# Recurrence of a linear-attention layer: squares of x in mid-chunk, roots by four, w_o loaded in part during the gate stage, seven PSUM banks for v and gate, the inverses' operand stored in their own order

## The chip, the cores and the metric

One core of one Trainium2 chip runs the whole program. The metric is device time in microseconds (us) of one execution.

## What is computed

A decoder trunk of two layers on x of 1024 tokens by 1024 channels, all in float32. The change lies in the first layer's time mixing, which works on the normalised input h with 16 heads of 64:

```python
x_r, x_w, x_k, x_v, x_a, x_g = h[None] + (x_prev - h)[None] * mu          # six mixes
r, k, v = x_r @ W_r, x_k @ W_k, x_v @ W_v
g = sigmoid(x_g @ g1) @ g2
def step(S, inp):                                 # for each token and head
    sa = einsum('bhvk,bhk->bhv', S, -kk_t)
    S = S * w_t + sa * b_t + v_t * k_t
    return S, einsum('bhvk,bhk->bhv', S, r_t)
...
y = groupnorm(y) * lnx_w + lnx_b
x = x + ((y + bonus) * g) @ w_o                   # residual
# next: h = rmsnorm(x), the first layer's MLP, ...
```

## The kernel before

The recurrence over 1024 tokens is done as 16 chunks of 64 tokens. Within a chunk the delta rule becomes a triangular system, whose 32x32 diagonal blocks are inverted beforehand. The order of the work is written out for most of the recurrence (`keep_in_program_order` pins an instruction to its engine's program order); in the projections a scheduler that simulates a timeline orders what is not pinned.

Up to about 230 us, the k projection (L824 products) runs beside *units* of preparation. Eight pairs of units, `prep_pair`, each make two 128x8x64 blocks of the matrix N (A_ab) from products of KK and BK, and SP stores each whole to the DRAM tensor `d_N` (L270, 256 KB, runs of 2 KB). `d_E`, `d_KR` and `d_BK` hold other prepared operands, of which `prep_receptance` loads `Er` and `kr` (L278, L281) again in the r projection (230 to 318 us, also L824).

`prep_inverse(b)`, b = 0 and 1, inverts half of the diagonal blocks each on DVE: 31 steps of two operations (L314, L316) on tiles `Nb`, `Tb`, `Tm`. Its operand `Nb` is gathered from `d_N` by 32 loads of 32 KB with runs of 128 bytes (L306), on the ACT queue for b = 0 and on SP for b = 1. The inverses stand beside the r projection (b = 0) and the v projection (L844, 318 to 417 us, b = 1). `mix(j)` makes the two halves (hi on ACT L730, lo on DVE L733) of a mixed input for each projection. The v projection's and the gate's products go to four PSUM banks (tile `mm`, pool `ps`); `psA`, three banks, is used by the units.

After the gate's first products (422 to 446 us) the recurrence runs. Chunk c solves (`pp`, copied by ACT to `Ps` L475, then `sa`, then `Z` on DVE L487), updates the state (`u`), makes its output `yp`, normalises and gates it, while blocks of the next chunk are prepared between. From chunk 3 on 24 products of w_o are filled into each chunk; they add a row block of 128 tokens (`xt`, L605) every second chunk. ACT then squares the row (L612, sum into `ssx`) and `rsqrt_small` makes the row's root (five DVE operations, L85 to L91, two ACT ones); both are issued after the second product of the next row, which places them ahead of `Ps` in chunks 5, 7, 9, 11, 13, 15 and once at the end.

A counter, `hook`, is called about seven times a chunk (hooks 0 to 6 before chunk 0, 7 to 13 in chunk 0, and so on) and lets other work in: steps of the gate's second product (table `GS`; tiles `gp`, copied by ACT L1124, stored to `d_g` by SP L1126), and the eight 128x1024 pieces of w_o. Piece i is loaded at hook 5 + 2i, and three hooks later ACT casts it (`woh`, L581) and POOL takes the difference (`wol`, L582). All eight thus fall in chunks 0 to 2.

Of the kernel before, what the change touches and what calls it, by code (L numbers as in the profile page):

```python
# [562 lines left out]
def stage_recurrence(k, a, tile_of, gates):  # L563
    nc, tc = k.nc, k.tc
    with ExitStack() as ctx:
        rec_pools(k, ctx, a)
# [8 lines left out]
        def load_wo(i):  # L575
            raw = k.rzz.tile([P, D], F32, tag="woraw", name="woraw", bufs=3)
            for q, hs in enumerate(HALF):
                tc.keep_in_program_order(nc.sync.dma_start(raw[hs], wv[i // 2, i % 2, q]))
# [4 lines left out]
            wo.append((hi, lo))
        xt, zs = [], []

        def w_out():

            done = None
            for tt in range(NK):
                zh, zl = zs[tt]  # L590
                for e in range(2):
# [14 lines left out]
                    if e == 1 and tt < NK - 1:  # L606
# [3 lines left out]
                        def done(tt=tt, zl=zl):  # L610
                            ss = k.rw.tile([P, 1], F32, tag="ssx", name="ssx")
                            nc.scalar.activation(zl.rearrange("p a b -> p (a b)"), xt[tt], AF.Square, accum_out=ss)  # L612
                            rsqrt_small(k, k.rw, k.rstd[tt], ss, 1.0 / D, 1e-6, tag="x")
# [14 lines left out]
        hooks, loads = 0, []  # L628
# [1463 lines left out]
```

## Time and profile before

| | us |
|---|---|
| three runs: lowest, median, highest | 2640.52, 2641.9, 2645.92 |
| the profiled execution: its time / its span | 2639.1 / 2637.4 |
| busy in the span: PE, DVE, ACT, POOL | 2537.5, 1852.2, 1237.6, 507.5 |
| recurrence, first to last chunk's products (462.13 to 757.89) | 295.76 |

The mean granted clock of TensorE is 0.983. PE is busy for 96% of the span, so time can only come from its gaps and from stretches at a lower clock. Lines of the first view below are stretches; a row of a timeline gives the start, the duration and, in brackets, for how long the engine was idle and what ended it.

### The profile page before, as it was taken

How to read it: one execution, taken by the hardware profiler on the slowest of the kernel's cores; microseconds unless marked ns; L12 is line 12 of the kernel's file. 1: busy time of each engine (PE TensorE's matmuls, PEld its weight loads, DVE VectorE, ACT ScalarE, POOL GpSimd, SP SyncE). 2: the span in 40 equal slices, each digit the busy share in tenths (PEclk: the TensorE clock that was granted, in tenths of full speed). 3: DMA queues.
4: the chain of work that ended last, by engine and by line, in shares of the span. 5: the costliest groups of instructions: out<-in, count | busy, mean ns of one | idle time of the engine just before them, and what ended most of it. 6: DMA issues, size and time to landing. Idle time of an engine off the chain costs nothing.

```text
span 2637.4 us, 44718 instructions
## 1 busy us (share of the span) xinstructions
PE 2537.5 (96%) x17601; PEld 2141.5 (81%) x17601; DVE 1852.2 (70%) x2982; ACT 1237.6 (47%) x2136; POOL 507.5 (19%) x395
## 2 busy tenths in 40 slices
PE   7999998799999999999999899999999999999999
PEld 4887897677778888888888899887887888878887
DVE  6665965788868777566778768587736877746675
ACT  4763324422355555443455424588715555543332
POOL 2011222866620000000301122344300000000020
PEclk9999999899999999999999999999999999999999
DMA  4468654966425544666641321755341644376664
GB/s 129 126 168 189 169 131 145 231 162 164 114 66 164 169 139 160 250 227 240 229 147 65 118 76 64 209 137 148 87 152 48 208 163 144 131 264 220 224 212 141
DMA packets 413510, 417.51 MB, mean 158 GB/s; under 512 B 189482, under 2 KB 297218, under 8 KB 413300
## 3 DMA queue, kind: packets, MB, share of 16 engines
q1 hardware_dynamic: 394068, 392.50, 49.0%
q0 software_dynamic: 4128, 12.66, 1.3%
q10 hardware_dynamic: 15104, 9.51, 1.2%
q8 instruction: 138, 2.26, 0.4%
q14 instruction: 72, 0.59, 0.1%
HBM read 292.76 MB, written 121.82 MB: 157 GB/s over the span
## 4 chain that ended last, share of the span: by engine, by line
PE 69%; DVE 15%; DMA 6%; issue 4%; ACT 3%; POOL 2%; SPq 1%; POOLq 0%; DVEq 0%; ACTq 0%
PE mm L365 34%; PE mm L768 7%; PE mm L766 7%; PE mm L767 7%; PE mm L824 4%; PE tp L368 2%; PE wo L365 1%; DVE Tb L316 1%; DMA b<-d_c 1%; PE s L365 1%; DVE Tm L314 1%; PE z1p L1001 1%; DVE AE L427 1%; PE o L365 1%; DMA R<-d_sm 1%
## 5 line engine op out<-in xcount | busy, mean ns | idle before, releaser
L365 PE MATMUL mm<-ol,oh 128*128 128x512 f32 x896 | 349.9, 391 | 1.3 <-DVE ol L733 1.3
L365 PE MATMUL mm<-oh 128*128 128x512 f32 x896 | 349.7, 390 | 1.3 <-ACT oh L730 1.3
L365 PE MATMUL mm<-oh,ol 128*128 128x512 f32 x896 | 349.9, 390 | 0.5 <-DVE ol L733 0.3
L730 ACT CAST oh<-ra 128x1024 fp32r<-128x1024 f32 x108 | 113.8, 1054 | 335.8 <-PE mm L365 237.5
L733 DVE TENSOR_TENSOR ol<-ra,oh 128x1024 fp32r<-128x1024 f32 x108 | 137.8, 1276 | 123.6 <-ACT oh L730 123.4
L365 PEld LDWEIGHTS mm<-ol,oh 128*128 128x128 f32 x896 | 168.9, 188 | 36.9 <-DVE ol L733 1.7
L365 PEld LDWEIGHTS mm<-oh,ol 128*128 128x128 f32 x896 | 168.9, 188 | 36.5 <-DVE ol L733 1.4
L365 PEld LDWEIGHTS mm<-oh 128*128 128x128 f32 x896 | 168.8, 188 | 36.5 <-ACT oh L730 1.7
L766 PE MATMUL mm<-xhT,ah 128*128 128x512 f32 x448 | 174.3, 389 | 0.0
L767 PE MATMUL mm<-xlT,ah 128*128 128x512 f32 x448 | 174.3, 389 | 0.0
L768 PE MATMUL mm<-xhT,al 128*128 128x512 f32 x448 | 174.3, 389 | 0.0
L1495 POOL DMA_DIRECT2D xt<-d_xh x8 | 4.4, 552 | 755.1 <-DMA rb<-in_mlp_w_out_dram 421.4
L730 ACT CAST ah<-w 128x512 fp32r<-128x512 f32 x128 | 79.3, 621 | 113.5 <-PE mm L767 102.1
L766 PE MATMUL mm<-xhB,ah 128*128 128x512 f32 x336 | 130.7, 389 | 0.0
L767 PE MATMUL mm<-xlB,ah 128*128 128x512 f32 x336 | 130.7, 389 | 0.0
L768 PE MATMUL mm<-xhB,al 128*128 128x512 f32 x336 | 130.7, 389 | 0.0
L733 DVE TENSOR_TENSOR ol<-rb,oh 128x1024 fp32r<-128x1024 f32 x92 | 120.8, 1313 | 2.1 <-ACT oh L730 1.8
L1811 ACT ACTIVATE l<-l,mx 128x512 f32<-128x512 f32 (+7 forms) x128 | 99.2, 776 | 34.3 <-DVE mx L1808 34.1
L1268 ACT ACTIVATE z<-z 128x512 f32<-128x512 f32 x112 | 70.8, 633 | 68.9 <-DVE z L1265 67.3
L767 PEld LDWEIGHTS mm<-xlT,ah 128*128 128x128 f32 x448 | 84.1, 188 | 17.6
L730 ACT CAST oh<-rb 128x1024 fp32r<-128x1024 f32 x92 | 96.4, 1048 | 4.0 <-DMA rb<-in_mlp_w_out_dram 4.0
L768 PEld LDWEIGHTS mm<-xhT,al 128*128 128x128 f32 x448 | 84.1, 188 | 17.4
(487 smaller groups left out, 6952.6 us busy)
## 6 DMA issues: line engine op xcount, KB each, us to landing
rb<-in_mlp_w_out_dram SPq DMA_DIRECT2D x124, 512.0 KB
ra<-d_H SPq DMA_DIRECT2D x108, 512.0 KB
w<-in_mlp_w_in_dram SPq DMA_DIRECT2D x64, 512.0 KB
d_H<-z SPq DMA_DIRECT2D x56, 512.0 KB
d_H<-sums SPq DMA_DIRECT2D x32, 768.0 KB
raw<-in_rwkv_w_rkv_dram SPq DMA_DIRECT2D x24, 512.0 KB
KRz<-d_KR SPq DMA_DIRECT2D x16, 512.0 KB
KRz<-d_BK SPq DMA_DIRECT2D x16, 512.0 KB
```

The costliest lines, as they stand in the source:

```text
L314: nc.vector.tensor_tensor(Tm[:, :, 0:n, 0:m], Nb[:, :, j, j + 1:32].unsqueeze(3).broadcast_to(S), Tb[:, :, j:j + 1, 0:m].broadcast_to(S), ...
L316: nc.vector.tensor_tensor(Tb[:, :, j + 1:32, 0:m], Tb[:, :, j + 1:32, 0:m], Tm[:, :, 0:n, 0:m], op=ALU.add)
L365: return self.tc.keep_in_program_order(self.tc.nc.tensor.matmul(*args, **kw))
L368: return self.tc.keep_in_program_order(self.tc.nc.tensor.transpose(*args))
L730: nc.scalar.copy(hi, src)
L733: lo_eng.tensor_tensor(lo, src, hi.bitcast(F32), op=ALU.subtract)
L766: te.matmul(out, ah, bh, start=i == 0, stop=False)
L767: te.matmul(out, ah, bl, start=False, stop=False)
L768: te.matmul(out, al, bh, start=False, stop=i == n - 1)
L824: nc.tensor.matmul(o[e][half], wt[:, i % 4, es], xs[i][part][:, 512 * half:512 * half + 512], start=i == 0 and wt is hi and part == 0, sto ...
L1268: nc.scalar.activation(x, x if o is None else o, AF.Relu)
L1811: nc.scalar.activation(l, l, AF.Exp, bias=m, scale=-1.0, accum_out=SM[:, j, qb:qb + 1])
```

## The change

- `d_N` becomes two tensors in the order in which `Nb` lies. `prep_pair` stores only the diagonal blocks, by eight stores of 32x8x32 (runs of 128 bytes) instead of two; `Nb` is one load on SP.
- The v products and the gate's first products rotate over seven banks (three of `psA`, four of `ps`).
- w_o's pieces follow a table `WO` of hooks. Pieces 1, 2, 3 have a pool of their own, the raw data of two of them is loaded in the gate stage, and they are converted at hooks 1, 3 and 5, ahead of chunk 0. Pieces 0, 5, 6 have their difference on POOL (hooks 10, 17, 24), 4 and 7 on DVE (hooks 21, 28).
- ACT loads its table at hook 9 instead of ahead of the `gp` copies, and stores `d_g` on its own queue.
- The squares of a row are issued once a chunk, between the state update and `rec_out`; roots are taken for rows 0 to 3 at once and for 4 to 6 at once.

```diff
-W0, WS, WL = 5, 2, 3
+WO = {1: (0, 1), 2: (0, 3), 3: (3, 5), 0: (5, 10), 4: (9, 16, 21), 7: (12, 23, 28), 5: (14, 17), 6: (18, 24)}
+EARLY = [1, 2, 3]
...
-    k.d_N = [dr.tile([P, HC, C], F32, name=f"d_N{i}") for i in range(2 * NK)]
+    k.d_N = [dr.tile([2, P, 32, 32], F32, name=f"d_N{i}") for i in range(2)]
...
-        nc.sync.dma_start(k.d_N[2 * p + h], N_)
+        u = 2 * (p % 4) + h
+        for c in range(2):
+            for d in range(2):
+                s0 = u % 4 * 32 + (c * 2 + d) * HC
+                q = 64 * c + 32 * d
+                nc.sync.dma_start(k.d_N[p // 4][u // 4, s0:s0 + HC].rearrange("c i t -> i c t"),
+                                  N_[q:q + 32, :, 32 * d:32 * d + 32])
...
-                (nc.sync if b else nc.scalar).dma_start(Nb[s0:s0 + HC, u // 4],
-                                  k.d_N[8 * b + u][q:q + 32, :, 32 * d:32 * d + 32].rearrange("i c t -> c i t"))
+    nc.sync.dma_start(Nb, k.d_N[b].rearrange("g s i t -> s g i t"))
...
-                            if done and (i, q) == (1, 2):
-                                done()
...
+        def squares():
+            while late:
+                tt, zl = late.pop(0)
+                tc.keep_in_program_order(nc.scalar.activation(zl..., xt[tt], AF.Square, accum_out=ss[:, tt:tt + 1]))
+                if tt in (3, 6):
+                    n = tt % 4 + 1
+                    rsqrt_small(k, k.rw1, k.rstd4[tt // 4][:, 0:n], ss[:, tt + 1 - n:tt + 1], 1.0 / D, 1e-6, tag=f"x{tt}")
...
+            if hooks == 9:
+                tc.keep_in_program_order(nc.scalar.preload_act_table_set("natural_log_exp_and_others"))
...
                     St = rec_state(k, cur, Z, Zn, St)
+            squares()
             rec_out(k, cur, Z)
...
-        fill(48)
+        fill(6)
+        squares()
+        fill(42)
+        k.wo_early.close()
...
+        def bank():
+            pool, tag = (k.psA, "psA") if next(turn) % 7 < 3 else (ps, "mm")
+            return pool.tile([P, 512], F32, tag=tag, name="mm")
...
+    k.woraw = [wo_raw(k, a, k.woe, i, 2, tc.keep_in_program_order) for i in EARLY[:2]]
...
-    pin(nc.scalar.preload_act_table_set("natural_log_exp_and_others"))
...
-                    nc.sync.dma_start(k.d_g[...], t)
+                    nc.scalar.dma_start(k.d_g[...], t)
```

ACT in a chunk in which a row of x is complete, before (`TT`: copies for the solve; `zl<-xt` the square; `rs_t`, `rstd` the root; `BKt`: copies for the state update; `ysq`: the squares of the normalisation):
```order
L464 COPY TT_4250<-op_6234 32x4x32 x4
L612 ACTIVATE zl,ssx<-xt_5230 128x1024
L475 COPY Ps<-pp 128x512
L86 ACTIVATE rs_t<-rs_v 128x1
L87 ACTIVATE rstd_72<-rs_t 128x1
L435 COPY BKt<-tp 128x512 x2
L533 ACTIVATE ysq<-Y 128x512
```
and in the same chunk of the change:
```order
L466 COPY TT_4230<-op_6200 32x4x32 x4
L477 COPY Ps<-pp 128x512
L437 COPY BKt<-tp 128x512 x2
L598 ACTIVATE zl,ssx<-xt_5205 128x1024
L535 ACTIVATE ysq<-Y 128x512
```
The square moved from ahead of `Ps` to behind both `BKt` copies, and the two root operations are gone from this chunk.

ACT from the gate's first half to chunk 0's `Ps`, before (`gp` is the product of the gate's second half):
```order
L1109 ACT_TABLE_LOAD
L1124 COPY xt_4302<-gp 128x512 x2
L435 COPY BKt<-tp 128x512
L1124 COPY xt_4322<-gp 128x512 x2
L1124 COPY gs<-gp 128x512
L435 COPY BKt<-tp 128x512
L1124 COPY gs<-gp 128x512 x4
L447 COPY O_4394<-op 128x128
L1124 COPY gs<-gp 128x512
L464 COPY TT_4247<-op_4420 32x4x32 x4
L475 COPY Ps<-pp 128x512
```
and the same place in the change:
```order
L1156 COPY xt_4283<-gp 128x512 x2
L437 COPY BKt<-tp 128x512
L1158 DMA d_g<-xt_4283 128x2x512
L1156 COPY xt_4307<-gp 128x512 x2
L1158 DMA d_g<-xt_4307 128x2x512
L584 CAST woh_4297<-woraw 128x1024
L1156 COPY gs<-gp 128x512
L437 COPY BKt<-tp 128x512
L1156 COPY gs<-gp 128x512
L1158 DMA d_g<-gs 128x2x512
L584 CAST woh_4299<-woraw 128x1024
```
The table load is gone from here, and three stores of `d_g` and the first two casts of w_o pieces stand among the `gp` copies.

DVE at the first inverse, before (`Er`, `kr`: the r projection's results; `KK<-np`: the last pair's N):
```order
L269 TENSOR_TENSOR KK<-np__2120,nt 128x512
L269 TENSOR_TENSOR KK<-np__2121,nt 128x512
L291 TENSOR_TENSOR Er<-mm,Er 128x8x64
L292 SCALAR_TENSOR_TENSOR kr<-Er,cols_443,kr 128x512
L291 TENSOR_TENSOR Er<-mm,Er 128x8x64
L292 SCALAR_TENSOR_TENSOR kr<-Er,cols_443,kr 128x512 x3
L291 TENSOR_TENSOR Er<-mm,Er 128x8x64 x2
L314 TENSOR_TENSOR Tm<-Nb,Tb 128x2x31
L316 TENSOR_TENSOR Tb<-Tb,Tm 128x2x31
L314 TENSOR_TENSOR Tm<-Nb,Tb 128x2x30x2
```
and in the change:
```order
L299 TENSOR_TENSOR Er<-mm,Er 128x8x64
L246 TENSOR_TENSOR Em<-kt,Em 128x512
L248 TENSOR_TENSOR BK<-Em,BK 128x8x64
L250 TENSOR_TENSOR BK<-Em,a 128x8x64
L316 TENSOR_TENSOR Tm<-Nb,Tb 128x2x31
L243 SCALAR_TENSOR_TENSOR KK<-kt,cols_429,E_593 128x512
L318 TENSOR_TENSOR Tb<-Tb,Tm 128x2x31
L316 TENSOR_TENSOR Tm<-Nb,Tb 128x2x30x2
L318 TENSOR_TENSOR Tb<-Tb,Tm 128x2x30x2
```
The first step on `Nb` came forward from behind the r projection's `Er` results to the middle of the last pair's units, ahead of its N.

## Rows read from the trace of the kernel before

**Rows 1.** Stretches of the recurrence, one from each chunk's first state product `pp` to the next chunk's: chunks 0 to 5, 7, 9, 11, 13 and the last. Columns: stretch, its length, then busy us and instructions of PE, PE's weight loads, DVE, ACT and POOL, the granted clock, the DMA share and GB/s.
```profile
462.13:477.07 14.94, 12.76 (x249) 10.29 (x240) 10.31 (x14) 6.15 (x13) 8.66 (x7) 0.90 0.97 243
477.07:497.82 20.75, 14.80 (x276) 12.24 (x277) 16.01 (x23) 8.94 (x19) 19.43 (x14) 0.91 1.03 240
497.82:520.90 23.08, 17.78 (x286) 15.20 (x277) 17.72 (x25) 7.75 (x18) 20.08 (x16) 0.73 1.00 222
520.90:537.86 16.96, 16.61 (x299) 13.69 (x293) 14.50 (x24) 5.10 (x14) 11.71 (x10) 0.97 0.75 219
537.86:553.76 15.90, 15.90 (x293) 13.11 (x293) 14.04 (x25) 4.70 (x14) 10.27 (x9) 1.00 0.54 132
553.76:573.75 19.99, 16.68 (x294) 13.49 (x293) 17.45 (x30) 5.87 (x18) 13.41 (x12) 1.00 0.66 188
...
589.65:608.83 19.18, 16.52 (x294) 13.42 (x293) 16.69 (x28) 5.64 (x16) 12.92 (x13) 1.00 0.68 194
...
624.73:643.81 19.08, 16.57 (x294) 13.48 (x293) 16.61 (x28) 5.46 (x16) 13.51 (x13) 1.00 0.61 167
...
659.71:679.58 19.87, 17.66 (x293) 14.61 (x293) 16.61 (x30) 6.60 (x20) 13.24 (x13) 0.91 0.51 136
...
696.38:714.68 18.30, 16.52 (x293) 13.42 (x293) 15.76 (x30) 6.56 (x20) 11.40 (x11) 1.00 0.39 89
...
730.58:757.89 27.31, 23.13 (x209) 18.77 (x208) 14.89 (x32) 7.61 (x18) 9.04 (x7) 0.88 0.07 16
```

**Rows 2.** Waits of PE from chunk 4 to the end of the recurrence (537 to 758 us). Columns: what waited for what, us in total, times, longest.
```profile
PE sa L365 <- ACT Ps L475: 10.0, 6, 2.2
```

**Rows 3.** ACT in chunk 7, in order of time. Columns: start, duration of the group, engine, line, operation, tiles, and in brackets the idle time before and what ended it.
```profile
592.59 1.06 ACT L612 ACTIVATE zl<-xt 128x1024 fp32r<-128x1024 f32 x1 [2.15 <-DVE xt L605]
...
593.76 0.59 ACT L475 COPY Ps<-pp 128x512 f32<-128x512 f32 x1
...
602.73 0.63 ACT L533 ACTIVATE ysq<-Y 128x512 f32<-128x512 f32 x1 [4.88 <-DVE Y L531]
```

**Rows 4.** DVE in chunk 7, same columns: the first and the last of the five operations of one row's root, and the operation behind them.
```profile
593.77 0.15 DVE L85 TENSOR_SCALAR rs_v<-ssx 128x1 f32<-128x1 f32 x1 [1.22 <-ACT zl L612]
...
595.58 0.93 DVE L91 TENSOR_TENSOR rstd<-rstd,rs_t 128x1 f32<-128x1 f32 x1
596.44 1.40 DVE L487 TENSOR_TENSOR Z<-sa,ns 64x512 f32<-64x512 f32 x2
```

**Rows 5.** Chunk 2, same columns: DVE, POOL, ACT and PE around 499 to 505 us (each row names its engine).
```profile
499.23 2.73 DVE L538 TENSOR_TENSOR Y<-Y,rsd 128x512 f32<-128x512 f32 x1
...
521.31 0.69 DVE L538 TENSOR_TENSOR Y<-Y,rsd 128x512 f32<-128x512 f32 x1
...
499.05 2.37 POOL L582 TENSOR_TENSOR wol<-woraw,woh 128x1024 fp32r<-128x1024 f32 x1
...
503.12 1.04 ACT L581 CAST woh<-woraw 128x1024 fp32r<-128x1024 f32 x1
...
504.83 1.97 PE L365 MATMUL sa<-Ps,TT 128*64 128x64 f32 x32 [2.68 <-ACT Ps L475]
```

**Rows 6.** DVE, ACT and PE where the inverses, the v product and the gate's first product meet, same columns.
```profile
361.67 0.27 DVE L314 TENSOR_TENSOR Tm<-Nb,Tb 128x62 f32<-128x62 f32 x1 [23.36 <-DMA Nb<-d_N]
...
318.78 0.55 PE L844 MATMUL mm<-whi,hi 128*128 128x256 f32 x1 [3.85 <-DVE Er L291]
...
421.56 1.05 ACT L961 COPY tv<-mm 128x512 f32<-128x512 f32 x2
...
449.84 1.28 ACT L1109 ACT_TABLE_LOAD   x1
...
422.18 0.80 PE L365 MATMUL mm<-hi,whi 128*128 128x512 f32 x1 [5.22 <-ACT tv L961]
```

**Rows 7.** Waits of PE between 410 and 462 us.
```profile
PE gp L365 <- ACT xt L1124: 1.8, 1, 1.8
```

**Rows 8.** Stretches of the projections (columns as in rows 1).
```profile
100.00:220.00 120.00, 117.77 (x918) 100.93 (x917) 71.20 (x120) 76.82 (x117) 12.96 (x15) 0.98 0.56 157
220.00:260.00 40.00, 36.11 (x287) 29.59 (x285) 18.21 (x32) 6.77 (x13) 5.64 (x9) 0.99 0.99 221
240.00:260.00 20.00, 16.11 (x80) 13.35 (x78) 4.57 (x7) 2.54 (x6) 2.84 (x2) 0.98 0.97 191
260.00:280.00 20.00, 20.00 (x91) 17.09 (x92) 18.86 (x33) 2.35 (x9) 4.46 (x2) 0.85 0.94 221
420.00:440.00 20.00, 17.82 (x69) 11.42 (x70) 8.80 (x10) 9.43 (x14) 5.82 (x10) 0.84 0.45 111
```

**Rows 9.** The ACT queue and PE at the loads of `Nb` for the first inverse (columns as in rows 3).
```profile
233.41 22.58 ACTq L306 DMA_DIRECT2D Nb<-d_N  x25
256.04 1.99 ACT L730 CAST whi<-raw 128x1024 fp32r<-128x1024 f32 x2 [23.41 <-DMA d_KR<-Er]
...
258.63 0.47 PE L824 MATMUL mm<-hi,whi 128*128 128x512 f32 x1 [2.05 <-ACT bon L209]
```

**Rows 10.** The tensor `d_N`: its loads and stores with shortest, median and longest ns of the issue and the first and last start.
```profile
L306 ACTq DMA_DIRECT2D Nb<-d_N x32: 271/272/1178, 225.2 to 255.6; - x32
...
L270 SPq DMA_DIRECT2D d_N<-KK x16: 325/599/1327, 101.1 to 241.9; - x16
```

**Rows 11.** The costliest groups of instructions (section 5 of the page): DVE's differences of 128x1024, with busy us and mean ns of one, then the idle time before.
```profile
L733 DVE TENSOR_TENSOR ol<-ra,oh 128x1024 fp32r<-128x1024 f32 x108 | 137.8, 1276 | 123.6 <-ACT oh L730 123.4
```

More of the change, by code (lines that the diff above doesn't have):

```diff
@@ L608, in w_out @@
                             tc.keep_in_program_order(nc.sync.dma_start(k.d_xh[tt * P:tt * P + P, :], xt[tt]))
[L610 to L613, printed above, removed]
+                        late.append((tt, zl))
                     yield
@@ L626, in fill @@
                 next(products, None)
[L628 removed]
+        hooks, loads = 0, {}
         def hook():
@@ L634, in hook @@
                 next(gates, None)
-            i = hooks - W0
-            if i >= 0 and i % WS == 0 and i // WS < NK:
-                loads.append(load_wo(i // WS))
-                next(loads[-1])
-            i -= WL
-            if i >= 0 and i % WS == 0 and i // WS < NK:
-                next(loads[i // WS], None)
+            if hooks == 9:
+                tc.keep_in_program_order(nc.scalar.preload_act_table_set("natural_log_exp_and_others"))
+            for i, at in WO.items():
+                if hooks == at[0]:
+                    loads[i] = load_wo(i)
+                if hooks in at:
+                    next(loads[i], None)
             hooks += 1
@@ L835, in proj_tokens @@
         pcs = [load_w(k, wv[:, 4 * q:4 * q + 4, 256 * g:256 * g + 256], [P, 4, 256], lo_eng=lo_eng) for q in range(2)]
-        os_ = [ps.tile([P, 2, 256], F32, tag="mm", name="mm") for _ in range(B)]
+        os_ = [bank().rearrange("p (j e) -> p j e", j=2) for _ in range(B)]
         for i, b in [(i, b) for i in range(NK) for b in range(B)] if g in (0, G - 1) else \
@@ L962, in emit_v @@
             nc.scalar.dma_start(k.d_v[256 * b:256 * b + 256, 256 * g:256 * g + 256].rearrange("(j t) e -> t j e", t=P), tv)
-        proj_tokens(k, ps, xv, wr[2], emit_v, nc.gpsimd)
+        turn = iter(range(P))
+        def bank():
+            pool, tag = (k.psA, "psA") if next(turn) % 7 < 3 else (ps, "mm")
+            return pool.tile([P, 512], F32, tag=tag, name="mm")
+        proj_tokens(k, bank, xv, wr[2], emit_v, nc.gpsimd)
         prep.close()
@@ L968, in stage_mix @@
         xg = mix(5)
+        k.wo_early = ExitStack()
+        k.woe = k.wo_early.enter_context(tc.tile_pool(name="r_we", bufs=1, side="right", reuse_waits="tile"))
+        k.woraw = [wo_raw(k, a, k.woe, i, 2, tc.keep_in_program_order) for i in EARLY[:2]]
         with tc.high_priority(offset=GP):
-            return gate(k, weights, xg, ps, tp_, tile_of)
+            return gate(k, weights, xg, bank, tp_, tile_of)
 def lora_weights(k, a, tp_):
@@ L1059, in lora_a, with wo_raw @@
     return t
+def wo_raw(k, a, pool, i, bufs, pin):
+    wv = a["rwkv_w_o"][0].rearrange("(j q h v) e -> j h q v e", q=2, h=2, v=C)
+    raw = pool.tile([P, D], F32, tag="woraw", name="woraw", bufs=bufs)
+    for q, hs in enumerate(HALF):
+        pin(k.nc.sync.dma_start(raw[hs], wv[i // 2, i % 2, q]))
+    return raw
 def gate_weights(k, a, tile_of):
@@ L1080, in gate_weights, with gate @@
     return ws, gh, gl, g3
-def gate(k, weights, xg, ps, tp_, tile_of):
+def gate(k, weights, xg, bank, tp_, tile_of):
     nc, pin = k.nc, k.tc.keep_in_program_order
@@ L1090, in gate @@
         s = slice(512 * half, 512 * half + 512)
-        os_ = [ps.tile([P, 512], F32, tag="mm", name="mm") for _ in range(2)]
+        os_ = [bank() for _ in range(2)]
         for i in range(NK):
```

38 lines of the change are left out of this document (20 added, 18 removed).

## The prediction

> **What bounds the kernel now.** I read the waits and busy times first over the whole span and then by stretches. PE is busy in 2537.5 of 2637.4 us, so the change is worth what it gives back of PE's gaps and of stretches at a lower clock, in the part that it touches (about 100 to 760 us). The recurrence is the best place to see this. A chunk in which nothing else happens takes 15.90 us with PE busy for all of it, at clock 1.00: chunk 4 [rows 1]. Every second chunk is longer: 19.99, 19.18, 19.08, 19.87 and 18.30 us in chunks 5, 7, 9, 11 and 13 [rows 1]. These are the chunks in which a row of x is squared. And chunks 1 and 2 take 20.75 and 23.08 us although they hold fewer products, with PE idle for 5.95 and 5.30 us and the clock at 0.91 and 0.73 [rows 1]. In both places PE's waits name ACT's copy `Ps` [rows 2, 5].
>
> **Part A, squares and roots.** In chunk 7 ACT starts the square at 592.59, for 1.06 us, and `Ps` only at 593.76 [rows 3], and `sa` waits for `Ps`. Then DVE makes the root's five operations between 593.77 and 596.51, 2.74 us from first start to last end (with a gap for ACT's two operations), and `Z`, which `u` waits for, starts at 596.44 behind them [rows 4]. So one row costs both ACT's and DVE's place on the chunk's chain of pp, Ps, sa, Z, u. The excess over 15.90 us is 4.09 + 3.28 + 3.18 + 3.97 + 2.40 = 16.9 us in chunks 5, 7, 9, 11 and 13. Chunk 15 squares a row as well, with no even neighbour of its kind to compare with; I give it the mean of the five, 3.4 us, which makes 20.3 us. Moved, the square stands behind the second `BKt` copy, ahead of `ysq`, where ACT was idle for 4.88 us [rows 3]: 1.06 us and the read of the sum fit there. If that cover were gone, `ysq` would be late by 1 us, and it is followed by the normalisation and not by the state. The roots' DVE work falls from seven times five operations to twice five, one set late in chunk 11 and one behind the last row but one, where products remain to be done. The ends: 10.0 us, the waits for `Ps` alone [rows 2], and 20.3 us. I take **-17**, near the upper end, because the even chunks show the same chain with no wait at all; the three us that I leave are for DVE's longer busy time in odd chunks, 16.6 on the mean against 14.0 us [rows 1], of which the five root operations are a part only.
>
> **Part B, w_o and the start of the recurrence.** Chunks 0 to 2 hold all eight pieces. POOL's difference takes 2.37 us, and DVE's `Y` operation that started beside it took 2.73 us, where it takes 0.69 us later [rows 5]: 2 us lost on DVE for one piece. ACT's cast, 1.04 us, stands directly ahead of `Ps` in chunk 2, and `sa` waited 2.68 us [rows 5]. Counting a full-clock chunk by its products, 15.90 us for 293 [rows 1], chunks 0 to 3 with 249, 276, 286 and 299 would take 13.5, 15.0, 15.5 and 16.2 us; they took 14.94, 20.75, 23.08 and 16.96, an excess of 15.5 us. The change leaves three pieces on POOL instead of eight, moves three ahead of chunk 0 and two differences to DVE (1.28 us each, as DVE's differences of 128x1024 take elsewhere [rows 11], in place of POOL's 2.37), and takes 1.5 MB of loads out of stretches where the DMA engines are at 0.97 to 1.03 [rows 1]. What it adds: eight stores of `d_g` on ACT's queue, two casts among the `gp` copies. A DMA issue that finds its turn taken can hold ACT; the nearest rows are the 25 `Nb` issues of 22.58 us, 0.90 us each [rows 9], so eight cost up to 7.2 us of ACT, of which those ahead of a `Ps` reach PE. The ends: -15.5 and +2 (no gain, and two of the issues and one cast in front of `Ps`). Removing five of eight pieces' interference is 0.6 of the excess: **-9**.
>
> **Part C, v and gate.** PE waits 3.85 us at the first v product for a bank that DVE's last `Er` result frees, and 5.22 us at the gate's first product for a bank that ACT's last `tv` copies free, which start only at 421.56 behind the gate's mix [rows 6]. With seven banks in turn both take a free bank. For the second it is also needed that the mix is ready. DVE makes it behind the second inverse, which stood still for 23.36 us for its 32 loads [rows 6]; with one load on SP it starts without that gap, so the mix comes earlier by up to as much. The 1.8 us that `gp` waits [rows 7] stand behind the table load of 1.28 us [rows 6], which moves into chunk 0, where ACT is busy for 6.15 of 14.94 us [rows 1]. The waits make 3.85 + 5.22 + 1.8 = 10.9 us; the clock of 0.84 over the 17.82 busy us after the second gap [rows 8] gives back up to 2.9 us. Ends: -3 (only the v wait, cut short by an earlier stop of the mix) and -13.8. I take **-10**: all three waits, less 1 us for what becomes late next, the last of the mix.
>
> **Part D, N and the first inverse.** ACT's queue spent 22.58 us on 25 of the 32 issues, and ACT's next operation came after 23.41 us idle, two us late for PE's next product, which waited for ACT's copy `bon` [rows 9]. PE lost 3.9 of the 20 us from 240 to 260, and ran at 0.85 in the 20 us behind it [rows 8], 3.0 us more. The change takes these 32 issues away and costs 6 more stores on SP for each pair. For pairs 0 to 5 they lie beside a k projection in which PE is busy for 117.77 of 120 us and the DMA engines for 0.56 [rows 8]: nothing, unless the third rival holds. For pairs 6 and 7 they lie where SP issues the `Er` and `kr` loads: 12 issues at 0.60 us [rows 10] are 7.2 us. Ends: -6.9 and +7.2; in the same stretch 32 issues go and 13 come, so **-3**.
>
> **Sum.** 17 + 9 + 10 + 3 = 39 us off the profiled execution's 2639.1, which is 2600.1. The median of the runs, 2641.9, is 2.8 us above that execution, so I forecast **2602.9 us** for the median. About 0.2% (5.3 us) is what a measurement of this kernel can tell from no change.
>
> **Rivals.**
>
> *DVE takes ACT's place.* In odd chunks DVE is busy 15.8 to 17.5 us [rows 1], near the 15.90 of a chunk. If the addition to `xt` and the normalisation, and not the roots, hold back `Z`, only the waits for `Ps` come back: 10 instead of 17, and with two w_o differences on DVE as well 4 instead of 9. Then it is 27 us, 2614.9. For it: 16.69 us in chunk 7 against 14.04 in chunk 4, 2.65 us more. Against it: the five root operations lie exactly between `sa` and `Z` [rows 4].
>
> *The small stores delay the first inverse.* In the changed order DVE's first step on `Nb` stands ahead of the last pair's N. If SP is behind, DVE stands still there, and the r projection's results with it. Part D is then +7.2 instead of -3, and 2613.1 us. For it: DMA share 0.99 from 220 to 260 us [rows 8]. Against it: the 32 loads of 128-byte runs are part of that share and are gone.
>
> *Slower: the stores bound the k projection.* Each pair now writes 8 x 32 x 8 = 2048 runs of 128 bytes instead of 256 of 2 KB. Before, 8192 such runs were read by the first inverse's loads; if they alone had filled the 40 us at share 0.99 [rows 8], a run would cost 4.9 ns of all engines together, and a pair 10.0 us. That is an upper bound, since they were 1.0 MB of the 8.8 MB that went through (221 GB/s). Free in a pair's period of 20.1 us (stores from 101.1 to 241.9 us in seven steps [rows 10]) is 0.44 of it, 8.8 us. So it starts to matter from 4.3 ns a run, and eats the whole gain when a pair needs 4.9 us more than that (39 over 8 pairs): 13.7 us, 6.7 ns a run, 1.4 times the bound. At 1.5 times the bound a pair needs 15.0 us, 6.2 over, 50 us in eight pairs: 2653 us. Nothing in the trace prices a write of 128 bytes, but it would have to cost well over what a read of this length can have cost. The Trainium skill speaks for this rival: its page "DMA: Bandwidth & Descriptors", section Specifications, says that transfers under 512 bytes make the DMA engine read, modify and write. By that page as an estimate, a write at twice the upper bound of a read is 20 us a pair and some 90 us more; the trace shows no case of it.
>
> *It comes to nothing.* The gain of the recurrence could be handed back at the MLP, if that waited for its weights and not for the rows. Then the time is about 2640. Against it: the DMA engines are at 0.07 in the last stretch [rows 1], so nothing is being waited for there.
>
> **How the numbers follow.** The forecast has 0.62, DVE in ACT's place 0.18, the late first inverse 0.13, slower 0.04, nothing 0.03. Faster by over 0.2% therefore 0.93, within 0.2% 0.03, slower 0.04. The range goes down to 2588, where A and B reach their ends with 20.3 and 13 and C and D 14 and 7 (54 us), and up to 2628, where both of the first two rivals hold (12 and 10 us less) and 3 us of C is missing.
>
> **What would show it.** Odd chunks of 16 to 17 us with the square between the `BKt` copies and `ysq`, and no root operations between `sa` and `Z` (A). Chunks 1 and 2 under 19 us (B). No wait of several us at the first v and gate products, and no gap of 23 us on DVE (C). PE busy for over 18 of the 20 us behind the last pair, and no `Nb` issues on ACT (D). It is wrong if PE waits in the k projection for stores, if odd chunks stay near 19 us, or if `Ps` waits for a store of `d_g`.

## The result and the profile after

| | before | after |
|---|---|---|
| median of four runs each (lowest to highest), us | 2641.8 (2640.52 to 2645.92) | 2622.0 (2619.39 to 2623.84) |
| the profiled execution: time / span | 2639.1 / 2637.4 | 2622.4 / 2620.7 |
| busy: PE, DVE, ACT, POOL | 2537.5, 1852.2, 1237.6, 507.5 | 2531.1, 1854.4, 1236.3, 508.1 |
| TensorE's mean granted clock | 0.983 | 0.987 |

The ratio of the times is 0.9923 [0.9904, 0.9943]: 20 us faster, inside the range (2588 to 2628), and half of the 39 us that the forecast summed up; between the two profiled executions it is 16.7 us. I cut the spans where PE begins a stage: **r** from the first k product to the first v product (k and r projections and the first inverse), **v** from there to the gate's first product, **gate** to chunk 0's first `pp`, then chunks 0 to 3, and chunk 4 to the first product of the first-layer MLP. The table, one profiled execution each, also carries the experiments of the next section; each ratio is against runs of the kernel before made beside that kernel (medians 2639.8 to 2641.8):

| kernel | r | v | gate | chunks 0 to 3 | chunk 4 to MLP | median of runs, ratio [95%] |
|---|---|---|---|---|---|---|
| before | 257.9 | 103.4 | 39.95 | 75.73 | 231.89 | 2641.8 |
| after | 263.94 | 96.17 | 37.74 | 73.66 | 221.63 | 2622.0, 0.9923 [0.9904, 0.9943] |
| sq_only | 258.99 | 102.36 | 39.96 | 76.55 | 219.75 | 2625.8, 0.9948 [0.9930, 0.9966] |
| vh2 | 263.06 | 96.18 | 37.75 | 77.80 | 221.98 | 2629.6, 0.9950 [0.9932, 0.9968] |
| vh_after | 258.80 | 96.44 | 37.76 | 74.64 | 214.91 | 2614.3, 0.9898 [0.9880, 0.9917] |
| wo_old | 263.93 | 96.18 | 36.80 | 78.35 | 220.89 | 2626.0, 0.9945 [0.9930, 0.9960] |
| nolo | 261.14 | 96.51 | 38.10 | 71.75 | 221.82 | 2620.0, one run |
| now | 263.79 | 96.19 | 37.02 | 69.76 | 219.27 | 2614.7, one run |
| bank4 | 263.85 | 96.36 | 38.61 | 75.42 | 220.69 | 2625.0, 0.9935 [0.9911, 0.9958] |
| n_act | 258.96 | 96.01 | 37.76 | 78.83 | 218.61 | 2622.0, 0.9926 [0.9909, 0.9943] |
| n_old | 254.74 | 101.91 | 42.40 | 73.68 | 220.55 | 2624.9, 0.9942 [0.9924, 0.9961] |
| inv_late | 252.24 | 101.77 | 40.61 | 71.69 | 221.99 | 2618.3, 0.9917 [0.9901, 0.9933] |
| inv_mid | 256.76 | 99.62 | 37.75 | 73.38 | 220.35 | 2616.5, 0.9907 [0.9889, 0.9925] |
| combo | 256.17 | 100.35 | 37.75 | 78.53 | 215.56 | 2615.6, 0.9905 [0.9889, 0.9920] |

The 16.7 us between the two spans are +6.0 in r (part D), -7.2 and -2.2 in v and gate (C), -2.1 in chunks 0 to 3 (B), -10.3 from chunk 4 on (A), +0.3 ahead of r and -1.2 from the MLP on. The letters are only roughly the prediction's: its wait of 3.85 us at the first v product, a term of C, lies at the end of r in this cut. The intervals of many kernels overlap, so what follows rests on stages and waits. A stage whose code kernels share still differs by up to 5 us in r and 7 us in chunks 0 to 3; a smaller difference there, part B's -2.1 among them, is not told from nothing.

**The chunks after** answer to [rows 1]: stretches from `pp` to `pp`, chunks 0 to 7, 9, 11 and 13, with length, busy us and instructions of PE, PE's weight loads, DVE, ACT and POOL, clock, DMA share and GB/s.
```profile
459.00:477.55 18.55, 13.91 (x251) 11.74 (x241) 11.55 (x15) 7.92 (x14) 11.66 (x9) 0.82 1.02 266
477.55:495.10 17.55, 13.76 (x285) 11.64 (x276) 14.22 (x23) 7.78 (x18) 13.16 (x12) 0.90 0.92 244
495.10:512.00 16.90, 13.90 (x287) 11.72 (x277) 15.30 (x20) 6.62 (x14) 11.55 (x9) 0.90 0.70 191
512.00:532.66 20.66, 17.35 (x302) 13.80 (x293) 19.66 (x30) 5.82 (x16) 15.76 (x13) 1.00 0.64 181
532.66:548.59 15.93, 15.93 (x294) 13.12 (x293) 13.97 (x24) 4.68 (x13) 11.29 (x10) 1.00 0.53 135
548.59:564.51 15.92, 15.92 (x293) 13.11 (x292) 14.65 (x25) 6.60 (x19) 10.10 (x9) 1.00 0.70 199
564.51:584.13 19.62, 17.77 (x293) 14.55 (x292) 14.53 (x23) 4.06 (x11) 11.60 (x11) 0.91 0.53 136
584.13:602.34 18.21, 16.31 (x294) 13.30 (x293) 14.53 (x23) 4.79 (x12) 13.48 (x13) 1.00 0.64 184
...
618.26:636.42 18.16, 16.33 (x293) 13.30 (x292) 14.48 (x23) 4.71 (x12) 13.38 (x13) 1.00 0.68 188
...
652.35:670.21 17.86, 16.51 (x293) 13.42 (x293) 15.68 (x27) 5.69 (x16) 13.40 (x12) 1.00 0.59 156
...
686.12:702.98 16.86, 16.24 (x294) 13.30 (x293) 14.61 (x24) 5.32 (x14) 12.04 (x11) 1.00 0.42 97
```
DVE in odd chunks fell to 14.5 to 15.7 us, as foreseen, but chunks 7, 9 and 11 still take 18 us with PE idle, and chunk 6, which had no excess of note, takes 19.62. Chunks 1 and 2 are shorter by 3.2 and 6.2 us, and chunks 0 and 3 longer by 3.6 and 3.7.

**PE's waits after**, from chunk 4 to the MLP (what waited for what, us, times, longest), answer to [rows 2]:
```profile
PE yp L367 <- POOL KRz L455: 8.9, 10, 1.3
PE yp L367 <- DVE Z L489: 1.2, 2, 0.8
```
and, of the same view before, one line that [rows 2] does not show:
```profile
PE yp L365 <- POOL KRz L453: 1.1, 1, 1.1
```
The 10.0 us for `Ps` are gone, and in their place `yp`, the product behind `pp`, waits 8.9 us for `KRz`, which POOL makes; before, that wait came once (in chunk 5).

**The projections after** answer to [rows 8], columns as above:
```profile
100.00:220.00 120.00, 117.77 (x921) 101.09 (x922) 71.18 (x120) 76.51 (x117) 12.93 (x15) 0.98 0.55 137
...
240.00:260.00 20.00, 16.68 (x66) 13.36 (x65) 15.77 (x25) 1.05 (x1) 1.42 (x1) 0.83 0.81 191
260.00:280.00 20.00, 15.42 (x72) 12.92 (x70) 18.18 (x24) 2.30 (x9) 3.38 (x2) 0.83 0.64 165
...
420.00:440.00 20.00, 20.00 (x94) 13.33 (x94) 9.02 (x9) 8.76 (x13) 6.40 (x10) 1.00 0.40 102
```
The k projection, with the small stores of pairs 0 to 5, is what it was, to 0.01 us. The 40 us behind it became worse (PE idle for 7.9 of 40 us, where it was 3.9). From 420 to 440 us, in the gate stage, PE has no gap and the full clock.

### The profile page after: what moved, and what is told of

It is laid out like the page before. It is cut to its first block, busy times and chain, and to the rows that moved or that the text cites. A ratio compares the mean times of both kernels' runs of the same rounds, so it can differ in the third digit from the quotient of the medians.

```text
span 2620.7 us, 44642 instructions
## 1 busy us (share of the span) xinstructions
PE 2531.1 (97%) x17601; PEld 2135.2 (81%) x17601; DVE 1854.4 (71%) x2959; ACT 1236.3 (47%) x2126; POOL 508.1 (19%) x393
## 4 chain that ended last, share of the span: by engine, by line
PE 77%; DVE 7%; issue 5%; DMA 4%; POOL 3%; ACT 2%; SPq 1%; POOLq 0%; DVEq 0%; ACTq 0%
PE mm L367 37%; PE mm L780 7%; PE mm L781 7%; PE mm L782 7%; PE mm L838 4%; PE mm L858 4%; PE tp L370 3%; PE s L367 2%; PE o L367 2%; PE wo L367 1%; PE z1p L1025 1%; PE sums L203 1%; POOL KRz L455 1%; DMA Vh<-d_v 1%; DMA b<-d_c 1%
## 5 line engine op out<-in xcount | busy, mean ns | idle before, releaser
L838 PE MATMUL mm<-hi,whi 128*128 128x512 f32 x256 | 89.0, 412 | 10.0 <-DVE Er L299 7.9
L780 PEld LDWEIGHTS mm<-xhT,ah 128*128 128x128 f32 x448 | 84.1, 188 | 17.4
```

What stands on the lines that cost most here:

```text
L780: te.matmul(out, ah, bh, start=i == 0, stop=False)
L838: nc.tensor.matmul(o[e][half], wt[:, i % 4, es], xs[i][part][:, 512 * half:512 * half + 512], start=i == 0 and wt is hi and part == 0, sto ...
```

## The experiments

All are the changed kernel with the edit shown, but for `sq_only`, which is the kernel before with one part of the change.

**sq_only: part A alone.** `rec_step`'s `late`/`squares()` and the grouped roots, put into the kernel before; nothing else.
```diff
+            squares()
             rec_out(k, cur, Z)
...
-        fill(48)
+        fill(6)
+        squares()
+        fill(42)
```


> The kernel before with the squares and the roots moved, and nothing else. Theory: the wait for Ps goes and KRz on POOL ends the chunk instead, as in the changed kernel; chunk 4 to the MLP takes 220 to 223 us instead of 231.9, and the time is 2630 to 2632. Rival: KRz is late because of the other parts (w_o, d_g on ACT's queue); then it takes 213 to 216 here, and the time is 2624.

Chunk 4 to the MLP took 219.75, 12.1 us less than before, as in the changed kernel, and r, v and gate stayed within 1.1 us of before. The whole is 0.9948 of before, two thirds of the gain of all four parts (2625.8 us, below the 2630 to 2632 expected). The new wait comes with it (PE's waits in that stretch, columns as above):
```profile
PE yp L365 <- POOL KRz L453: 8.0, 9, 1.3
```
So part A itself uncovered `KRz`; neither w_o nor the early loads made it late.

**vh2: two `Vh` tiles.** On POOL `KRz` stands behind `Vh` and `St`. Chunk 7 of the changed kernel, start, duration, engine, line, operation, and idle time ahead:
```profile
580.64 1.06 POOL L543 TENSOR_TENSOR Vh<-Vh,bon 128x512 f32<-128x512 f32 x1 [5.71 <-DMA Vh<-d_v]
581.66 2.66 POOL L508 TENSOR_TENSOR St<-Z,sc 64x512 f32<-64x512 f32 x2
584.13 1.15 PE L367 MATMUL pp<-Z,AE 128*64 128x64 f32 x32
584.39 3.06 POOL L455 TENSOR_TENSOR KRz<-KRz,sc 64x512 f32<-64x512 f32 x2
586.03 0.32 PE L367 MATMUL yp<-Z,KRz 64*64 64x64 f32 x2 [0.75 <-POOL KRz L455]
587.50 1.14 PE L367 MATMUL yp<-Z,KRz 64*64 64x64 f32 x30 [1.15 <-POOL KRz L455]
```
POOL sits idle for 5.71 us until the load of `Vh` lands, then runs `Vh`, `St` and `KRz` in one go, and `KRz` ends at 587.45, 3.3 us behind the start of `pp`. In chunk 8 the load lands 5.45 us ahead of `pp` instead of 3.49, and `yp` does not wait. The load can only start when the chunk before is done with the one `Vh` tile, so a second tile should let it come early.
```diff
-    V = w1.tile(S3, F32, tag="Vh", name="Vh")
+    V = w.tile(S3, F32, tag="Vh", name="Vh")
```
(`Ps` gives up its second buffer for the room.)

> The changed kernel with two tiles for Vh (the v rows that the normalisation adds) and one instead of two for Ps, whose room that takes. Theory: in the odd chunks KRz is late on POOL because it stands behind Vh, and Vh's only tile is loaded after its last use, in the next chunk; with two tiles POOL no longer idles 3 to 6 us for the load, PE's waits yp <- KRz (8.9 us after 532 us) fall below 2 us, chunks 7, 9, 11 take 16 to 16.5 us instead of 18, and the kernel some 8 us less than the changed one: 2614. Rival: POOL itself is short of time (13 of 18 us busy) or DVE is; then the waits change their name and the time stays at 2622.

The waits for `KRz` stayed, 8.5 us in 10 times, the stretch took 221.98, and the time was 2629.6 us where 2614 had been expected. The test failed to test it: with the second tile the program places `Vh`'s multiplication one chunk earlier on POOL, where it waits for a load that starts no earlier against its place in the queue than before. It neither bears the theory out nor speaks against it.

**vh_after: `Vh` held behind `KRz` on POOL.** No new buffer, only the order.
```diff
-    nc.gpsimd.tensor_tensor(V, V, k.bon[:, :, c:c + 1].broadcast_to(S3), op=ALU.mult)
-    nc.gpsimd.tensor_tensor(Y, Y, V, op=ALU.add)
+    def bonus():
+        ...
+    return bonus
...
+            with tc.issue_after(k.krz.ins) if more else nullcontext():
+                bonus()
```


> The changed kernel with POOL's multiplication of Vh held behind its KRz of the same chunk (it stood ahead of St and KRz, and POOL idled there 3 to 6 us for Vh's load). Theory: KRz is late because of this order alone; PE's waits yp <- KRz (8.9 us after 532 us) fall below 2 us, the way from chunk 4 to the MLP's first product goes from 221.6 to 213 or 215 us, and the time is 2613 to 2616. Rival: POOL or DVE is short of time as such; another wait comes in its place (zp <- Y, or Z), the way stays at 219 to 222, the time at 2620 to 2622.

POOL in chunk 6 (columns as in chunk 7 above):
```profile
566.78 1.29 POOL L546 TENSOR_TENSOR Y<-Y,Vh 128x512 f32<-128x512 f32 x1
568.04 2.18 POOL L508 TENSOR_TENSOR St<-Z,sc 64x512 f32<-64x512 f32 x2
570.29 2.19 POOL L455 TENSOR_TENSOR KRz<-KRz,sc 64x512 f32<-64x512 f32 x2
572.56 1.06 POOL L545 TENSOR_TENSOR Vh<-Vh,bon 128x512 f32<-128x512 f32 x1
```
`St` and `KRz` now run ahead of `Vh`. PE's largest wait from chunk 4 to the MLP is
```profile
PE op L367 <- DVE AE L429: 3.4, 10, 0.4
```
and none is for `KRz`. The stretch takes 214.91 us (before 231.89), and the time is 2614.3 us, 0.9898 of before: the lowest median of all, though its interval overlaps that of other kernels. That turning the order alone takes the wait away shows its cause. The chunks do not all fall to 15.9: most take 16.5, with up to 0.4 us for `AE` in ten of them. The whole stretch (columns as in the chunk rows), of after and then of this kernel:
```profile
532.66:754.29 221.63, 211.45 (x3477) 173.48 (x3477) 184.72 (x299) 74.40 (x181) 141.47 (x116) 0.99 0.49 128
```
```profile
527.26:742.17 214.91, 210.18 (x3477) 172.39 (x3477) 167.03 (x297) 73.45 (x178) 127.73 (x116) 1.00 0.51 132
```
With the same work, DVE was busy for 17.7 and POOL for 13.7 us less: other operations now run beside each other. On the mean `KRz` went from 1.36 to 1.08 us, `St` from 1.34 to 1.05, DVE's `zl` from 1.24 to 0.75; DVE's `m` became longer, 0.17 to 0.63.

**wo_old, nolo, now: w_o.** `wo_old` puts the old hooks back, so that all eight pieces are converted in chunks 0 to 2; `nolo` replaces the eight differences by zeroing the tile (the low parts of w_o are left out); `now` leaves out w_o's preparation altogether, loads, casts and differences (the products use one zero tile).
```diff
-WO = {1: (0, 1), 2: (0, 3), 3: (3, 5), 0: (5, 10), 4: (9, 16, 21), 7: (12, 23, 28), 5: (14, 17), 6: (18, 24)}
-EARLY = [1, 2, 3]
+WO = {i: (5 + 2*i, 8 + 2*i) for i in range(8)}
+EARLY = []
```
```diff
-                nc.gpsimd.tensor_tensor(lo, raw, hi.bitcast(F32), op=ALU.subtract)
+                nc.gpsimd.memset(lo.bitcast(F32), 0.0)
```
```diff
+            wo[i] = (zero, zero)
+            yield
```


> The changed kernel with w_o's pieces at the hooks of before (all eight in chunks 0 to 2, all differences on POOL). Theory: the new table is worth little, as chunks 0 to 3 took 72 to 79 us in five kernels with it and 75.7 before; they take 74 to 78 here, and the time is 2621 to 2625. Rival: the table is worth the 9 us that I forecast; then they take over 80, and the time is above 2629.

> The changed kernel without the eight differences of w_o: the low halves are set to zero by POOL instead, which writes only. Theory: what is left of chunks 0 to 3's excess is DVE held up beside POOL's differences, and DVE's own two; chunks 0 to 3 take 64 to 67 us instead of 73.7, and the pair of AE operations on DVE goes from 2.9 to 4.5 us to under 2. Rival: it is ACT's casts and the loads; then they take 71 to 74.

> The changed kernel without any preparation of w_o: no loads, no casts, no differences; one tile of zeros stands for all sixteen halves, and the products are all still done. Theory: chunks 0 to 2 have no products of w_o to fill PE's waits, so their length is that of their own chain, and my reckoning by the number of products gave it an excess that no arrangement of w_o can return; chunks 0 to 3 still take 65 to 70 us (73.7 in the changed kernel). Rival: the excess is w_o's work; then they take 60 to 62.

Chunks 0 to 3 took 78.35, 71.75 and 69.76 us, beside 73.66 after; `nolo` thus stayed far above the 64 to 67 expected. `now`, a single run, is the nearest to a lower bound: here the first and the last of its chunks 0 to 3:
```profile
457.77:472.32 14.55, 11.81 (x249) 9.61 (x240) 10.40 (x20) 6.54 (x15) 6.51 (x7) 0.93 0.95 263
...
507.74:527.53 19.79, 18.27 (x300) 14.64 (x293) 15.82 (x24) 4.53 (x12) 14.23 (x13) 0.91 0.70 202
```
With no w_o work at all these chunks are still 9.6 us over the 60.2 that I had counted from their products, and PE's largest wait there is
```profile
PE op L367 <- DVE AE L429: 6.7, 8, 2.2
```
The same wait is the largest of chunks 0 to 3 before and after as well:
```profile
PE op L365 <- DVE AE L427: 5.8, 7, 2.3
```
```profile
PE op L367 <- DVE AE L429: 8.4, 7, 3.4
```
So of before's 75.73 us all of w_o's preparation is worth some 6.0 by this one run, a size within the spread of 7 us, and I had taken back 9 from it. What the table alone is worth is not settled: `wo_old` is 4.7 us slower there than after, but the nine kernels with the table and all of its work run from 71.7 to 78.8, and those without it are 75.73, 76.55 and 78.35.

**bank4: v and gate on four banks.**
```diff
-            pool, tag = (k.psA, "psA") if next(turn) % 7 < 3 else (ps, "mm")
+            pool, tag = (ps, "mm")
```


> The changed kernel with v's and the gate's products on four banks as before. Theory: seven banks removed the waits at the first v product (3.85 us before) and at the gate's first (5.2 before), since both wait for a bank; the first gate product comes 4 to 9 us later against the r projection's start than in the changed kernel, and the time is 2626 to 2630. Rival: the earlier inverses removed them, since DVE and ACT are then done early; the time stays at 2620 to 2623.

v took 96.36 us and gate 38.61, 0.2 and 0.9 more than after, and the first v product waits 1.7 us where after it waits for nothing. PE's waits at the gate and at the first v product, which answer to [rows 6]:
```profile
PE mm L367 <- ACT tv L975: 1.0, 2, 0.6
...
PE mm L858 <- DVE Er L299: 1.7, 1, 1.7
```
The gap of 5.22 us stays away with the old four banks. What removed it is DVE, which is done with the second inverse when the gate's mix is to be made. DVE in the changed kernel at 399.55:
```profile
399.55 1.23 DVE L747 TENSOR_TENSOR wlo<-raw,whi 128x1024 fp32r<-128x1024 f32 x1 [21.86 <-ACT whi L744]
```
It had been idle for 21.86 us; before, the last step of that inverse ended only at 407.79, behind its gap of 23.36 us [rows 6], and the mix ran from there to beyond PE's arrival.

**n_act, n_old: the stores of N.** `n_act` gives the N stores of the last two pairs to ACT's queue; `n_old` is before's two whole stores for each pair and 32 loads for each inverse.
```diff
-                nc.sync.dma_start(k.d_N[p // 4][u // 4, ...
+                (nc.scalar if p > 5 else nc.sync).dma_start(k.d_N[p // 4][u // 4, ...
```


> The changed kernel with the 16 small stores of N of the last two pairs on ACT's queue, which stands idle from 231 to 257 us, instead of SP's. Theory SP: the loads of Er and kr come late because 7 us of store issues stand ahead of them on SP; then they are issued some 7 us earlier, the first v product starts at 318 to 319 us instead of 325, and the kernel takes 2616. Theory DVE: the r results are late because the inverse's steps stand among them; then the first v product stays at 323 to 325 and the time at 2620 to 2622.

> The changed kernel with N stored whole and gathered by 32 loads for each inverse, as before; all else as changed. If the new storage is what costs the 6 us in the r projection, the first v product comes at 315 to 319 us (318.8 before, of which 3.85 was a wait for a bank that seven banks take away). The second inverse then waits again for its loads, about 23 us; if that is what the gate's gap hung on, the gate's first product waits for its mix by up to 5 us, and the kernel takes 2618 to 2622; if the seven banks alone removed the gap, 2614.

`n_act`: r took 258.96, 5 us less than after, which is no more than kernels with the same r differ by (258.8 to 263.9), and the whole time did not move (2622.0); it settles nothing. (ACT's queue was held for 10.2 us by eight of the stores, and the last pair came late by that.) `n_old`: r 254.74, 9.2 less, but v 101.91 and gate 42.40, 10.4 more; with seven banks and the old loads the gain of part C is gone. Together with `bank4` this shows that part C hangs in the main on the loads and stores of N, and little on the banks. Nor is it only r's loss given back: `vh_after` and `n_act` begin v as early as `sq_only` does (r 258.8 to 259.0) and need 96.0 to 96.4 us for it, `sq_only` 102.4.

**inv_late, inv_mid: the first inverse's steps held back.** In `inv_late` the 31 steps stand behind the sixth `kr`, in `inv_mid` one group of r products sooner.
```diff
-            if e == 1:
+            if e == 2:
...
+    with nullcontext() if b else k.tc.issue_after(k.last_kr.ins):
         for j in range(31):
```
(`inv_mid` keeps `e == 1`.)

> The changed kernel with the first inverse's steps on DVE held back behind the kr result of the second pair of the r projection, about where they began before. Theory DVE: PE's 7.9 us of waits for Er go, the first v product starts at 317 to 319 us, and the kernel takes about 2616, less if the second inverse is still early enough for the gate. Theory SP: DVE then waits for the loads of Er and kr themselves, the first v product is at 322 to 325, and the time 2620 to 2624.

> The changed kernel with the first inverse's steps held behind the fourth kr result of the r projection, two results sooner than in inv_late. Theory: the 6 us in the r projection come from the steps among its first results, and 5 us of the v part in inv_late come from the second inverse starting too late; in between both are mostly saved: r projection 253 to 256 us, v part (first v product to the gate's first) 96 to 98, time 2613 to 2616. Rival: the two are one price that only moves; r and v parts together stay at 354 to 356, and the time at 2618.

`inv_late`: r 252.24, 11.7 less than after and 5.7 less than before, so the steps among the first `Er` results are where r loses its time. The `kr` loads are late here too: the group of six begins 187.5 us behind the first k product, where it is 188.4 after and 184.2 before. Late loads alone thus do not lengthen r. But v is 5.6 and gate 2.9 longer: the second inverse now starts later, behind a wait of its own.
```profile
361.65 0.28 DVE L317 TENSOR_TENSOR Tm<-Nb,Tb 128x62 f32<-128x62 f32 x1 [14.33 <-POOL Tb L312]
```
`inv_mid` lies between (256.76 and 99.62). r, v and gate together are 394.6 and 394.1, after 397.9, before 401.3: holding the steps back keeps 3 to 4 us of the 12 and pays the rest back in v and gate. Even these stay within the spread (`vh_after`, without this edit: 393.0).

**combo: vh_after and inv_late, with two `Nb` tiles,** so that the second load need not wait.
```diff
-    Nb, Tb, Tm = (k.pi.tile([P, 2, 32, 32], F32, tag=n, name=n) for n in ("Nb", "Tb", "Tm"))
+    ... bufs=2 if n == "Nb" else 1 ...
```


> The changed kernel with Vh behind KRz (as vh_after), the first inverse behind the sixth kr result (as inv_late), and two tiles for Nb, so that the second inverse need not wait for the first to be done before its load is issued. Theory: the gains add; r projection 252 to 255 us, v part 96 to 98, chunk 4 to the MLP 214 to 216; time 2605 to 2609. Rival: the v part keeps the 5 us that inv_late lost there, because DVE's work is then too late as a whole; time 2611 to 2614, no better than vh_after.

2615.6 us, not told apart from `vh_after`, and not the 2605 to 2609 expected. From chunk 4 on it keeps 215.56; r and v are near `inv_mid`, and chunks 0 to 3 took 78.53.

## Why the prediction was right, and where not

**Part A (-17; measured -10.3).** The mechanism was right. ACT in chunk 7 after, which answers to [rows 3]:
```profile
585.33 0.58 ACT L477 COPY Ps<-pp 128x512 f32<-128x512 f32 x1 [0.74 <-PE pp L367]
592.03 0.59 ACT L437 COPY BKt<-tp 128x512 f32<-128x512 f32 x1 [2.17 <-PE tp L370]
592.51 1.06 ACT L598 ACTIVATE zl<-xt 128x1024 fp32r<-128x1024 f32 x1
```
`Ps` starts right behind `pp`, the square 7 us later, and DVE's busy time in odd chunks fell from 16.6 to 14.8 us on the mean. The step that failed is the reason for taking the value near the upper end, "the even chunks show the same chain with no wait at all". By POOL's rows they had no wait because the odd chunks were long. `KRz` for chunk 7 and for chunk 8, before:
```profile
587.43 2.74 POOL L453 TENSOR_TENSOR KRz<-KRz,sc 64x512 f32<-64x512 f32 x2
...
604.17 2.60 POOL L453 TENSOR_TENSOR KRz<-KRz,sc 64x512 f32<-64x512 f32 x2
```
The first is made in a chunk of 15.9 us and ends 0.5 us behind the start of chunk 7's `pp` (589.65 [rows 1]), still in time for `yp`; the second is made in a chunk of 19.18 us and ends 2.1 us ahead of chunk 8's. After, with chunks 4 and 5 both at 15.9, `KRz` ended 1.8 us ahead of chunk 4's `pp`, 0.8 us behind chunk 5's and 3.3 us behind chunk 6's, and there `yp` waited. So POOL's row of `Vh`, `St` and `KRz` came some 2.5 us later with each chunk of 15.9 us, and the longer chunks gave that back. I had asked of every stall what is late next on ACT and DVE, but not on POOL, whose work before `pp` starts with a load.

`vh_after` has 231.89 - 214.91 = 17.0 us, but that this equals the -17 is in part luck. From chunk 4 to chunk 14 `vh_after` gained 11.2 us (after: 5.3), where I had counted 16.9; from chunk 15 to the MLP it gained 5.8 (after: 5.0), where I had counted 3.4.

**Part B (-9; measured -2.1).** The mis-sized term is the excess of 15.5 us, reckoned from products at 15.90 us for 293. A chunk with fewer products is not shorter in proportion: chunks 0 to 2 lack the w_o products that elsewhere fill PE's waits, so the chain through `AE` shows (6.7 us of waits with w_o's preparation left out). I had read one wait for `Ps` there [rows 5] and not the list: before, `AE` cost 5.8 us and `Ps` 2.9. The part of w_o is some 6.0 of the 15.5 (one run of `now`), and 0.6 of that is 3.6. Whether the table gained anything is not shown, since kernels with it took 71.7 to 78.8 us and before took 75.73. The other foreseen price did not come: a store of `d_g` held ACT for 0.37 to 0.42 us. A cast still stands ahead of `Ps`, now in chunk 0:
```profile
459.76 1.05 ACT L584 CAST woh<-woraw 128x1024 fp32r<-128x1024 f32 x1 [1.79 <-DMA woraw<-in_rwkv_w_o_dram]
462.27 0.58 ACT L477 COPY Ps<-pp 128x512 f32<-128x512 f32 x1
462.91 2.01 PE L367 MATMUL sa<-Ps,TT 128*64 128x64 f32 x32 [2.16 <-ACT Ps L477]
```
A part of the work moved to chunk 0, and its wait with it.

**Part C (-10; measured -9.4 in v and gate, more by its own terms).** Both gaps went, the clock from 420 to 440 rose from 0.84 to 1.00 (20.00 of 20.00 us busy), and `gp` waits 1.3 us in place of 1.8. But the -9.4 does not hold the wait of 3.85 us at the first v product, which this cut counts in r and which is gone too. `bank4` still waits 1.7 us there, so the banks took 1.7 to 3.85 of it, and C is -11.1 to -13.3, near its end of -13.8. What the -10 left out is the clock: PE was busy 2.2 us less in v and 1.7 less in gate, at 1.00 instead of 0.96 and 0.95. The reason is right by half. I asked for both a free bank and an early mix; in v and gate the banks are worth 1 us (`bank4`), and the second inverse that is over in time the rest: where it is late, with the old loads (`n_old`) or behind a later first inverse (`inv_late`), v takes 101.8 to 101.9 again.

**Part D (-3; measured +6.0).** The sign was wrong. With the 1.7 to 3.85 us that r gained at the first v product put to C, D is +7.7 to +9.9. Of the 3.9 us that I laid to the issues on ACT, 2.05 were the wait for `bon` [rows 9] and the rest a wait for a result of DVE:
```profile
PE mm L824 <- DVE Er L291: 1.8, 1, 1.8
```
The waits of PE at the r projection after:
```profile
PE mm L838 <- DVE Er L299: 7.9, 2, 4.6
```
and, from the timeline, what led to the second of them:
```profile
234.42 0.27 DVE L316 TENSOR_TENSOR Tm<-Nb,Tb 128x62 f32<-128x62 f32 x1 [0.62 <-DMA Nb<-d_N]
...
249.52 6.52 SPq L289 DMA_DIRECT2D kr<-d_BK  x6
...
258.58 2.38 POOL L747 TENSOR_TENSOR wlo<-raw,whi 128x1024 fp32r<-128x1024 f32 x1 [26.05 <-ACT whi L744]
258.65 2.86 DVE L300 SCALAR_TENSOR_TENSOR kr<-Er,cols,kr 128x512 f32<-128x512 f32 x1 [1.60 <-DMA kr<-d_BK]
261.29 2.42 POOL L747 TENSOR_TENSOR wlo<-raw,whi 128x1024 fp32r<-128x1024 f32 x1 [0.33 <-ACT whi L744]
261.44 2.82 DVE L316 TENSOR_TENSOR Tm<-Nb,Tb 128x510 f32<-128x510 f32 x1
...
264.90 0.68 DVE L299 TENSOR_TENSOR Er<-mm,Er 128x512 f32<-128x512 f32 x1
265.73 0.76 PE L838 MATMUL mm<-hi,whi 128*128 128x512 f32 x1 [4.58 <-DVE Er L299]
```
SP's six `kr` loads are issued at 249.52, 4.5 us later than before (245.06), behind the last pair's stores; DVE waits for one of them; a step of the inverse stands ahead of the `Er` that PE needs, and takes 2.82 us beside POOL's difference. The second rival had the results of r late, but by another way: DVE was to stand still at the first step on `Nb`, and it waited there for 0.62 us. What costs the time is the steps themselves, which now stand among the first results (without them there, r is 11.7 us shorter); the prediction gave them no price. The rival's +7.2 was a price of store issues, so that it comes near is luck. The late loads are not shown to cost anything: in `inv_late` they are nearly as late, and in `n_act`, with no store of the last two pairs on SP, they are issued 188.2 us behind the first k product, as late as after. What the stores cost by themselves stays open, and the kernels with this r have between +0.9 and +6.0 in the cut.

**The rivals.** *DVE takes ACT's place* did not come from chunk 4 on, where DVE held back `Z` for 1.2 us; only in chunks 0 to 3 was DVE (`AE`) PE's largest wait, as it had been before. *The stores bound the k projection* is refuted: PE is busy for 117.77 of 120 us as before, at DMA share 0.55. The Trainium skill, page "DMA: Bandwidth & Descriptors", section Specifications, has transfers under 512 bytes read, modified and written; in PE's time no price of that is to be seen here. The packets tell what such a write took: between 100 and 220 us 12288 packets of 128 bytes took 9.7 us of the 16 engines together, 0.79 ns each, where the rival needed 4.3; before, 1536 packets of 2 KB, twice the bytes, took 8.5 us. *It comes to nothing* is refuted: what was gained ahead of the MLP was kept to the end (-1.2 us from the MLP on).

**The sum.** That the time lies in the range is in part luck. Its upper end was built from the first two rivals and 3 us of C. What came instead is 7 us less in A through `KRz`, which no rival named, 7 us less in B from a mis-sized excess, and 9 us or more the other way in D; C gave more than its term.

## What to carry to other kernels

When an operation leaves a chain, look up the second latest input of every product on it, on all engines, and how much later it may come: here POOL's `KRz` was on time only because every second chunk was long, and cost 8.9 us of waits until POOL's order was turned. A stretch that lacks filling work must not be priced by its count of products; leave the suspect out altogether, and take that as the most it can give. Where a helper's steps get earlier, look for who stands behind them on that engine: the inverse's early steps paid for v and gate (-9.4 us) with the r projection (+6.0).

## What the hardware showed beside that

- Order on POOL changes how long DVE's and POOL's operations take. Between the kernels after and `vh_after` a pair of `KRz` operations went from 3.06 to 2.19 us in the rows above, and DVE's busy time by 17.7 of 184.7 us, with the same work. The operation of 0.69 us that took 2.73 beside one of POOL's in [rows 5] looks like the same effect.
- The granted clock behind a wait of the same length is not the same in two kernels. In r a wait of 4.58 us ends at 265.73 after and at 261.91 in `vh_after`, whose code for this stage is the same. The stretch from 260 to 280 has 0.83 after (row above), and in `vh_after` 0.91:
```profile
260.00:280.00 20.00, 18.09 (x86) 15.26 (x87) 16.42 (x27) 0.64 (x4) 0.00 (x0) 0.91 0.74 183
```
  The waits ahead of it were not alike (3.32 and 2.38 us). This fits the spread of 5 us in r between kernels with the same code; it was not tested by itself.
- Beside the k projection the stores of six pairs, eight each of 256 runs of 128 bytes, cost PE nothing that can be measured (117.77 of 120 us); their packets took 0.79 ns each of all 16 DMA engines together.
